# Hybrid block on one core: the index projections of the third and fourth group of tokens placed between the other projections

## The chip, the core and the metric

The kernel runs on one core of a Trainium2 chip. A core has five engines that run their own instruction streams and wait for each other through semaphores: TensorE (PE, matmuls; the loading of the stationary operand is shown apart as PEld), VectorE (DVE), ScalarE (ACT), GpSimd (POOL) and SyncE (SP, whose queue issues nearly all DMAs, in order). Matmul results land in PSUM banks, from which VectorE or ScalarE must read them before the bank is used again. All other tiles lie in SBUF. The metric is the time of one execution on the device in microseconds, less is better.

## What is computed

One layer of a streaming encoder on 2048 tokens of 1024 channels. The part that matters here is the combined input projection and the indexer:

```python
proj = x @ w_in[l]
q, c_kv, q_idx, w_idx, k_idx, pool_in, gate_logits = jnp.split(proj, PROJ_SPLITS, axis=-1)
q = apply_partial_rope(q.reshape(B, S, N_HEADS, D_LATENT), cos_q, sin_q)
k_lat = apply_partial_rope(c_kv, cos_q, sin_q)
q_idx = apply_partial_rope(q_idx.reshape(B, S, IDX_HEADS, IDX_DIM), cos_i, sin_i)
k_idx = apply_partial_rope(k_idx, cos_i, sin_i)
# per block of 128 queries:
rel = jax.nn.relu(jnp.einsum('bqhd,bsd->bqhs', qib, k_idx) * idx_scale)
idx_score = jnp.einsum('bqh,bqhs->bqs', wib * head_w_scale, rel)
_, sel = lax.top_k(jnp.where(admissible, idx_score, -inf), 256)
# pooling branch, gates
branch_b = multiscale_pool(pool_in, w_pool, pool_scale) @ w_pool_branch
gate_a, gate_b = jnp.split(jax.nn.sigmoid(gate_logits), 2, axis=-1)
```

Behind it come attention over the 256 selected keys of each query, the two branches under their gates, an output projection with layer norm, and a feed-forward part with a short convolution.

## The kernel before

All products are made in nearly full precision: each operand is split into a high and a low part (`split`: a rounded copy, then a subtraction), and `mm3` issues three matmuls, high by high, high by low and low by high. A split runs on ScalarE and VectorE, or with `pool=True` on GpSimd, in pieces of 256 columns.

Tokens are handled in four groups of 512 (`NG = 4`), each of four row blocks of 128. The projections run in these stages:

- *Index* (`proj_index`), per group: latent keys, index queries, index weights and index keys, 712 columns in three column thirds of 256, 256 and 200. x comes in four pairs of channel blocks; each pair is loaded, split, used for the first third and stored to DRAM in split form. Pair 0 of the next group is split ahead (`split_ahead`). The weights of all three thirds are loaded and split once (`Weights` object `wi`) and held in `wi_parts` over all four groups. `finish_index` makes the rotary part of keys and index queries on VectorE (tiles `rope`). `keys` transposes the keys on TensorE: eight transposes of 128x128 against `ident`, from which the index keys go to `kst`.
- *Pooling* (`proj_pool`), *queries* (`proj_q`) and *gates* (`proj_gates`), per group, in this order, from the stored x (`load_parts`). Their weights are split on GpSimd for group 0, kept in DRAM as `wp`, and only loaded for groups 1 to 3 (`self.ab`). `store_q` transposes the finished query rows; two pieces of each group are still to be transposed when gates begin. `pool_map` multiplies the four pooled channel groups by `wpool`: three matmuls each, then ScalarE and VectorE empty the bank. The pooled maps are used in the second half of gates.

Before, the order is: index 0, 1, 2, 3, then pooling, queries and gates of group 0, of group 1, of group 2 and of group 3, then attention. `keys` of a group is called behind the second third of the next index group; that of group 3 at the second step of group 0's pooling.

Beside these stages runs background work (`scores_and_selection`): for groups 0 and 1 together, then 2, then 3, index scores (matmuls of queries with `kst`, relu on ScalarE, weighted sums on VectorE) and the selection, a search for the threshold by bits with counts on VectorE and ScalarE, then the masks. It can begin for a set when `keys` of its last group has been called (`keyed`). `turn`, called at every step of a stage, lets it go on while a planned clock of VectorE and ScalarE is at most `SLACK` = 3 us behind TensorE's. A Tile scheduler then fixes each engine's order within these bounds. Four PSUM banks (`PS1`) serve the projections; SBUF has 42 slots of 4 KB per partition (`T`) for weights, x, scores and rows alike.

All instructions carry the line number of a wrapper (L153), so that groups are told apart by tile names and shapes.

Of the kernel before, what the change touches and what calls it, by code (L numbers as in the profile page):

```python
# [65 lines left out]
GROUPS = ((0, 1), (2,), (3,))  # L66
P1AT = (2, 2)
# [28 lines left out]
LASTK = 6  # L96
SCAN = 1.04
# [162 lines left out]
class Kern:  # L260
    def __init__(self, ctx, tc, a, out):
        self.clocks = Clocks()
        self.tc, self.nc, self.a, self.out = tc, PacedCore(tc.nc, self.clocks), a, out
        self.stores, self.older, self.bg, self.late = [], [], [], []
        self.const = ctx.enter_context(tc.tile_pool(name="const", bufs=1))
        self.big = ctx.enter_context(tc.tile_pool(name="big", bufs=42))
        self.mid = ctx.enter_context(tc.tile_pool(name="mid", bufs=8))
        self.sm = ctx.enter_context(tc.tile_pool(name="sm", bufs=4))
        self.early_pool = tc.alloc_tile_pool(name="early", bufs=1)
        self.late_pool = None  # L270
        self.p1 = ctx.enter_context(tc.tile_pool(name="p1", bufs=4, space=PSUM))
        self.p2 = ctx.enter_context(tc.tile_pool(name="p2", bufs=2, space=PSUM))
        self.dram = ctx.enter_context(tc.tile_pool(name="dram", bufs=1, space=bass.MemoryType.DRAM))
        self.n, self.shared = 0, True
        self.credit = self.seen = 0.0
# [156 lines left out]
    def setup(self):  # L432
# [28 lines left out]
        def cols(c0, n):  # L461
# [5 lines left out]
        self.wi = Weights(self, [cols(C_IDX, 256), cols(C_IDX + 256, 256), cols(C_IDX + 512, 200)], pool=False,  # L467
                          first=True)
# [86 lines left out]
    def proj_index(self, g, done):  # L555
# [3 lines left out]
        self.rows[g] = rows  # L559
        for c in range(3):  # L560
            if g == 0:
                self.wi_parts.append(self.wi.get(c))
            w = self.wi_parts[c]
            n = 256 if c < 2 else 200
            if c == 0:
# [7 lines left out]
                for _ in self.split_x(g, use):  # L573
                    if n == (XAT if g else 3) and g + 1 < NG:
                        self.load_x(g + 1)
                    n += 1
                    yield
                if g + 1 == NG:
                    self.ab.split(0)
                    self.load_parts(0, range(NFIRST))  # L580
            for rb in range(RB):
                if c == 0:
                    ps = accs[rb]
                else:
                    if (c, rb) == P1AT and g + 1 < NG:
# [17 lines left out]
            if c == 1 and done:  # L603
                done()

# [146 lines left out]
    def pool_map(self, g):  # L752
        nc = self.nc
        self.pm = []
        for k in range(4):
            t = self.pooled[k]
            ps = self.PS1()
            self.mm3(ps, self.wpool[:, 0, k], self.wpool[:, 1, k], t[:, 0], t[:, 1], True, True)
            o = self.T([P, 2, G], F32R)
            sc = self.pscale[:, k:k + 1]  # L760
            nc.scalar.activation(o[:, 0], ps, AF.Identity, scale=sc)
            nc.vector.scalar_tensor_tensor(o[:, 1], ps, sc, o[:, 0].bitcast(F32), op0=OP.mult, op1=OP.subtract)
            self.pm.append(o)
            yield 0.7

    def proj_gates(self, g):
        nc = self.nc
        base = g * self.nab + 6
        for j in range(4):
# [7 lines left out]
            for i in range(2):  # L777
# [9 lines left out]
                yield 5.2  # L787
        for j in range(4):
            w = self.ab.get(base + 4 + 2 * j)
            if j == 2:  # L790
                if g + 1 < NG:
                    self.load_parts(g + 1, range(NPRE))
                else:
                    self.attn_load()
# [5 lines left out]
            for i in range(2):  # L800
# [9 lines left out]
                yield 5.2  # L810
            if j == 3 and g + 1 < NG:
                self.load_parts(g + 1, range(NPRE, DC // 2))
# [1026 lines left out]
    def run(self):  # L1839
        self.qpend, self.rows, self.wi_parts, self.keyed, self.selected = [], {}, [], -1, 1  # L1840
# [9 lines left out]
        self.wi.raw[0] = [self.wi.load_one(0, 0)]  # L1850
        self.load_x(0, range(1, 2))
        self.wi.raw[0].append(self.wi.load_one(0, 1))
        self.load_x(0, range(2, DC // 2))
        self.split_ahead(0, 1)
        self.wi.split(0)
# [4 lines left out]
        for g in range(NG):  # L1860
            self.run_to_end(self.proj_index(g, done))
            while self.spill:
                self.store(*self.spill.pop(0))
            done = self.finish_index(g)
        self.load_parts(0, range(NFIRST, DC // 2))
        for g in range(NG):
            for i, step in enumerate(self.proj_pool(g)):
                if i == 1 and g == 0:
                    done()
                    self.wi_parts = None  # L1870
                self.turn(step)
            self.run_to_end(self.proj_q(g))
            self.run_to_end(self.proj_gates(g))
# [38 lines left out]
```

## Time and profile before

| | |
|---|---|
| time, three runs | median 3289.72 us (3289.57 to 3299.82) |
| time of the profiled execution | 3292.94 us |
| its span, from the first to the last instruction | 3291.2 us |
| mean granted TensorE clock | 0.982 |
| DMA | 745.68 MB, of it read from HBM 514.36 MB, written 228.23 MB |
| matmuls | 15918 |

The span is what the trace shows between the first and the last instruction; the execution's own time has 1.7 us around it. Windows of the trace are given in microseconds from the start of the span. A row of such a table has, for each engine, its busy time and its number of instructions, then the granted TensorE clock (1.00 is full speed) and the share of the DMA engines.

### The profile page before, as it was taken

The page shows a single profiled execution, that of the slowest core. Times are in us where ns is not written, and L with a number is a line of the kernel's source. Part 1 is how long each engine was busy: PE and PEld are TensorE (multiplying, and loading weights), DVE is VectorE, ACT ScalarE, POOL GpSimd, SP SyncE. Part 2 cuts the span into 40 slices and gives each one's busy share as a digit, 9 for nine tenths or more (in the row PEclk, how much of TensorE's full clock was granted, in tenths as well). Part 3 has the DMA queues.
Part 4 walks back from the last instruction along what each step waited for, and adds up shares of the span by engine and source line. Part 5 has one row for each costly group of instructions (what it writes and reads, how often), then busy time and mean ns, then how long its engine had stood idle before and what let it go on. Part 6 is the DMA issues. An engine that isn't in the chain of part 4 may idle for free. (4 is left out here: it accounts for less than half of the span.)

```text
span 3291.2 us, 46503 instructions
## 1 busy us (share of the span) xinstructions
PE 3157.8 (96%) x15918; PEld 2654.2 (81%) x15918; DVE 2417.7 (73%) x4271; ACT 1559.4 (47%) x2656; POOL 1279.9 (39%) x1314
## 2 busy tenths in 40 slices
PE   8988899999999899999999999999999999999998
PEld 8877688898898788788878877777778778888787
DVE  5588859986988777777766666666688865555797
ACT  3466537846777466666621133333343433222443
POOL 3139411020010688766641143443166511121673
PEclk9999899999999899999999999999999999999999
DMA  8457565653665444434464459899797665566984
GB/s 327 148 199 275 191 251 195 246 203 136 227 226 194 144 172 172 157 130 161 157 224 147 156 186 320 309 327 339 288 380 264 208 252 224 224 238 246 364 296 163
DMA packets 325675, 745.68 MB, mean 227 GB/s; under 512 B 30074, under 2 KB 115006, under 8 KB 325438
## 3 DMA queue, kind: packets, MB, share of 16 engines
q1 hardware_dynamic: 315646, 724.88, 61.5%
q10 hardware_dynamic: 9792, 17.83, 1.4%
q8 instruction: 126, 2.06, 0.3%
q14 instruction: 111, 0.91, 0.1%
HBM read 514.36 MB, written 228.23 MB: 226 GB/s over the span
## 5 line engine op out<-in xcount | busy, mean ns | idle before, releaser
L153 PE MATMUL p<-b,b 128*128 128x512 f32 (+3 forms) x12644 | 2783.7, 369 | 56.1 <-ACT b L153 24.4
L153 PEld LDWEIGHTS p<-b,b 128*128 128x128 f32 x12644 | 2175.7, 191 | 453.0 <-ACT b L153 25.0
L153 ACT ACTIVATE b<-p 128x512 fp32r<-128x512 f32 (+9 forms) x726 | 427.7, 612 | 653.6 <-PE p L153 627.0
L153 ACT ACTIVATE b<-b 128x1024 fp32r<-128x1024 f32 (+2 forms) x248 | 253.6, 1028 | 390.7 <-POOL b L153 136.4
L153 DVE TENSOR_TENSOR b<-b,b 128x1024 fp32r<-128x1024 f32 (+6 forms) x246 | 369.6, 1541 | 42.6 <-ACT b L153 39.8
L153 ACT ACTIVATE m<-b,F 128x1024 bf16<-128x1024 f32 (+3 forms) x352 | 345.8, 985 | 68.0 <-DVE F L153 43.8
L153 DVE TENSOR_SCALAR_CACHE_REDUCE m<-b,F 128x768 bf16<-128x768 f32 (+4 forms) x374 | 346.8, 949 | 11.8 <-DMA q<-m 9.9
L153 POOL TENSOR_TENSOR b<-b,b 128x256 fp32r<-128x256 f32 (+3 forms) x276 | 314.1, 1152 | 101.7 <-ACT b L153 84.9
L153 DVE TENSOR_TENSOR m<-m,p 128x512 f32<-128x512 f32 x176 | 120.3, 684 | 242.8 <-ACT b L153 182.6
L153 POOL TENSOR_TENSOR m<-b,b 128x512 f32<-128x512 f32 x99 | 140.2, 1425 | 337.4 <-issue 258.6
L153 DVE SCALAR_TENSOR_TENSOR b<-b,cw,b 128x1023 f32<-128x1023 f32 (+1 forms) x176 | 245.0, 1392 | 26.2 <-ACT b L153 25.1
L153 DVE TENSOR_TENSOR b<-p,b 128x512 fp32r<-128x512 f32 (+1 forms) x286 | 201.7, 714 | 72.3 <-ACT b L153 69.7
L153 POOL TENSOR_SCALAR b<-b 128x256 fp32r<-128x256 f32 (+3 forms) x216 | 125.8, 596 | 325.6 <-DMA b<-in_w_in_dram 122.8
L153 PE MATMUL p<-b 128*128 128x512 f32 x616 | 235.1, 393 | 5.8 <-ACT b L153 4.0
L153 POOL TENSOR_TENSOR b<-b,m 128x512 f32<-128x512 f32 x110 | 192.0, 1760 | 123.8 <-DMA m<-in_w_ffn_down_dram 74.0
L153 PE MATMUL p<-ident,b 128*128 128x128 f32 x1456 | 213.1, 274 | 24.8 <-ACT b L153 13.5
L153 DVE CUSTOM_DVE_ANT_0 b<-p,b 128x1024 f32<-128x1024 f32 (+7 forms) x192 | 174.2, 909 | 65.8 <-PE p L153 64.5
L153 PEld LDWEIGHTS p<-ident,b 128*128 128x128 f32 x1456 | 174.2, 141 | 58.7 <-ACT b L153 16.5
L153 ACT ACTIVATE b<-b,mx 128x1024 f32<-128x1024 f32 (+7 forms) x192 | 171.5, 896 | 69.7 <-DVE mx L153 63.7
L153 ACT ACTIVATE m<-p 128x512 f32<-128x512 f32 (+1 forms) x180 | 104.9, 594 | 193.6 <-PE p L153 178.9
L153 DVE SCALAR_TENSOR_TENSOR b<-b,ws,b 128x768 f32<-128x768 f32 (+5 forms) x154 | 159.8, 1065 | 40.6 <-ACT b L153 38.6
L153 PE MATMUL p<-kst,b 128*128 128x384 f32 (+3 forms) x656 | 150.6, 359 | 4.1 <-ACT b L153 2.6
(130 smaller groups left out, 2360.8 us busy)
## 6 DMA issues: line engine op xcount, KB each, us to landing
b<-uw SPq DMA_DIRECT2D x308, 512.0 KB, 6.5
b<-wp SPq DMA_DIRECT2D x192, 512.0 KB, 5.8
uw<-l SPq DMA_DIRECT2D x98, 512.0 KB, 3.0
b<-in_w_ffn_down_dram SPq DMA_DIRECT2D x154, 256.0 KB, 5.3
b<-h SPq DMA_DIRECT2D x154, 256.0 KB, 5.3
wp<-b SPq DMA_DIRECT2D x64, 512.0 KB, 5.2
uw<-b SPq DMA_DIRECT2D x56, 512.0 KB, 3.5
h<-m SPq DMA_DIRECT2D x110, 256.0 KB, 5.9
```

The lines of the kernel that those rows point to most:

```text
L153: return f(*args, **kw)
```

## The change

The list `STAGES` sets the order now: index 0 and 1, the other projections ("mix") of group 0, index 2, mix 1, index 3, mix 2, mix 3. As the index weights are no longer held, they are loaded and split again for index 2 and index 3, on GpSimd (`pool=g > 0`). `load_x` and the first splits of x for these groups are called in the second half of the gates ahead of them, and the loads of the stored x for the next pooling inside and behind them. The key transposes that precede a pooling stage come at its sixth step (`KEYS_AT = 5`), the query transposes left over at the second and third of the first four gate projections' weights, and the four pooling maps one at a time behind the gate projections number 4 to 7 (`PM_AT`). While projections run, every fourth split that was meant for GpSimd goes to ScalarE and VectorE (`self.turns % 4`).

```diff
+STAGES = (("index", 0), ("index", 1), ("mix", 0), ("index", 2), ("mix", 1), ("index", 3), ("mix", 2), ("mix", 3))
+KEYS_AT = 5
+PM_AT = (4, 5, 6, 7)
...
-        if pool:
+        self.turns += 1
+        if pool and (not self.shared or self.turns % 4):
...
-        self.wi = Weights(self, [cols(C_IDX, 256), cols(C_IDX + 256, 256), cols(C_IDX + 512, 200)], pool=False,
-                          first=True)
+        index = [cols(C_IDX, 256), cols(C_IDX + 256, 256), cols(C_IDX + 512, 200)]
+        self.wi = {g: Weights(self, index, pool=g > 0, first=g == 0)
+                   for (kind, g), before in zip(STAGES, (None,) + STAGES) if kind == "index" and before != (kind, g - 1)}
...
+        straight = after == ("index", g + 1)
         for c in range(3):
-            if g == 0:
-                self.wi_parts.append(self.wi.get(c))
+            if g in self.wi:
+                self.wi_parts[c] = self.wi[g].get(c)
...
-                if g + 1 == NG:
-                    self.ab.split(0)
-                    self.load_parts(0, range(NFIRST))
+                if not straight:
+                    if after[1] == 0:
+                        self.ab.split(0)
+                    self.load_parts(after[1], range(NFIRST))
...
+            if not straight:
+                self.wi_parts[c] = None
...
+    def pool_map(self, k):
+        t = self.pooled[k]
+        ps = self.PS1()
+        self.mm3(ps, self.wpool[:, 0, k], self.wpool[:, 1, k], t[:, 0], t[:, 1], True, True)
...
-            if j == 3:
-                yield from self.pool_map(g)
-            if self.qpend and j < 2:
+            if self.qpend and 1 <= j < 3:
                 self.store_q()
...
-                yield 5.2
+                if 2 * j + i + 1 in PM_AT:
+                    yield 2.6
+                    self.pool_map(len(self.pm))
+                yield 2.6
...
-                if g + 1 < NG:
-                    self.load_parts(g + 1, range(NPRE))
+                if g + 1 == NG:
+                    self.attn_load()
+                elif after[0] == "index":
+                    self.load_x(after[1])
+                    self.wi[after[1]].load(0)
                 else:
-                    self.attn_load()
+                    self.load_parts(g + 1, range(NPRE))
...
+                if after[0] == "index":
+                    self.wi[after[1]].split(0)
+                    self.split_ahead(after[1], 1)
+                else:
+                    self.load_parts(g + 1, range(NPRE, DC // 2))
...
-        for g in range(NG):
-            self.run_to_end(self.proj_index(g, done))
-            while self.spill:
-                self.store(*self.spill.pop(0))
-            done = self.finish_index(g)
-        self.load_parts(0, range(NFIRST, DC // 2))
-        for g in range(NG):
+        for (kind, g), after in zip(STAGES, STAGES[1:] + (None,)):
+            if kind == "index":
+                self.run_to_end(self.proj_index(g, done, after))
+                while self.spill:
+                    self.store(*self.spill.pop(0))
+                done = self.finish_index(g)
+                if after[0] == "mix":
+                    self.load_parts(after[1], range(NFIRST, DC // 2))
+                continue
             for i, step in enumerate(self.proj_pool(g)):
-                if i == 1 and g == 0:
+                if i == KEYS_AT and done:
                     done()
-                    self.wi_parts = None
+                    done = None
```

How this moves instructions is seen in each engine's order. The first place is TensorE at the pooling maps of group 0. In the names `p` is a PSUM bank, `b` a slot of SBUF, `wpool` the pooling map's weights. Before:

```order
L153 MATMUL p_1140_4540<-b_2861,b_4298 128x512
L153 MATMUL p_1140_4540<-b_2862,b_4298 128x512
L153 MATMUL p_1140_4540<-b_2861,b_4299 128x512
L153 MATMUL p_1168_4631<-b_3338,wpool_586 128x512 x3
L153 MATMUL p_1171_4641<-b_3516,wpool_586 128x512 x3
L153 MATMUL p_1178_4662<-b_3745,wpool_586 128x512 x3
L153 MATMUL p_1180_4669<-b_4032,wpool_586 128x512 x3
L153 MATMUL p_1184_4681<-b_2210,b_4459 128x512
```

Now, at the first of them:

```order
L156 MATMUL p_834_3158<-b_1414,b_2914 128x512
L156 MATMUL p_834_3158<-b_1413,b_2915 128x512
L156 MATMUL p_853_3223<-b_2000,wpool_586 128x512 x3
L156 MATMUL p_866_3255<-ident_84,b_2689 128x128 x4
L156 MATMUL p_868_3263<-ident_84,b_2689 128x128 x4
L156 MATMUL p_870_3271<-b_1066,b_3051 128x512
L156 MATMUL p_870_3271<-b_1067,b_3051 128x512
```

Four maps in a row, each with a bank of its own, have become one map between two gate projections; behind this first one stand query transposes, and the next map follows 24 matmuls later.

The second place is TensorE at key transposes ahead of a pooling stage (`ident` against `m`). Before, behind index 3, where the three matmuls are the last of 24 of group 0's pooling:

```order
L153 MATMUL p_700_2898<-b_2853,b_2190 128x512
L153 MATMUL p_700_2898<-b_2854,b_2190 128x512
L153 MATMUL p_700_2898<-b_2853,b_2191 128x512
L153 MATMUL p_701_2923<-ident_84,m_2763 128x128
L153 MATMUL p_702_2924<-ident_84,m_2764 128x128
```

Now, behind index 2, where they are the last of 48 of group 1's pooling:

```order
L156 MATMUL p_1369_5102<-b_5089,b_4254 128x512
L156 MATMUL p_1369_5102<-b_5090,b_4254 128x512
L156 MATMUL p_1369_5102<-b_5089,b_4256 128x512
L156 MATMUL p_1374_5176<-ident_84,m_4991 128x128
L156 MATMUL p_1375_5177<-ident_84,m_4992 128x128
```

The transposes stand 24 matmuls later than they did, behind index 2 and behind index 3 alike.

The third place is VectorE at the start of index 2, which is now behind the gates of group 0. The first row is the last product of these gates (`m`), the last is the split of index 2's second x pair; between them stand rows of the selection of groups 0 and 1 (`F` the threshold, `c` the counts, the others small working tiles), shown in part:

```order
L156 TENSOR_TENSOR m_4433<-p_1236_4451,m_4433 128x512
L156 SCALAR_TENSOR_TENSOR ab_4548<-t_4549 128x2
L156 TENSOR_SCALAR m_4762,c_4734<-b_2082,F_4471 128x896
L156 TENSOR_SCALAR ab_4548<-ab_4548 128x2
L156 SCALAR_TENSOR_TENSOR ab_4785<-F_4471 128x4
...
L156 TENSOR_TENSOR t_4786<-t_4786,ab_4785 128x4
L156 TENSOR_SCALAR tn_4787<-t_4786 128x4
L156 TENSOR_TENSOR b_4518<-b_4036,b_4517 128x1024
```

Before, the splits of index 2's four x pairs stood together among the rotary rows of index 1:

```order
L153 TENSOR_TENSOR rope_1311<-b_924,cos_547 128x16
L153 TENSOR_TENSOR rope_1313<-b_924,sin_548 128x16
L153 TENSOR_TENSOR b_1246<-b_960,b_1245 128x1024
L153 TENSOR_TENSOR b_1404<-b_962,b_1403 128x1024
L153 TENSOR_TENSOR b_1440<-b_964,b_1439 128x1024
L153 TENSOR_TENSOR b_1476<-b_966,b_1475 128x1024
```

The second to fourth of these splits moved from there to behind a gate product and 14 rows of selection.

More of the change, by code (lines that the diff above doesn't have):

```diff
@@ L553, in rope, with proj_index @@
         nc.vector.tensor_tensor(o2, ts[2], ts[3], op=OP.add)
-    def proj_index(self, g, done):
+    def proj_index(self, g, done, after):
         nc = self.nc
@@ L573, in proj_index @@
                 for _ in self.split_x(g, use):
-                    if n == (XAT if g else 3) and g + 1 < NG:
+                    if n == (XAT if g else 3) and straight:
                         self.load_x(g + 1)
@@ L584, in proj_index @@
                 else:
-                    if (c, rb) == P1AT and g + 1 < NG:
+                    if (c, rb) == P1AT and straight:
                         self.split_ahead(g + 1, P1N)
@@ L750, in lazy_step, with proj_gates @@
             self.lazy.pop(0)()
-    def pool_map(self, g):
+    def pool_map(self, k):
         nc = self.nc
[L754 to L766, printed above, removed]
+        t = self.pooled[k]
+        ps = self.PS1()
+        self.mm3(ps, self.wpool[:, 0, k], self.wpool[:, 1, k], t[:, 0], t[:, 1], True, True)
+        o = self.T([P, 2, G], F32R)
+        sc = self.pscale[:, k:k + 1]
+        nc.scalar.activation(o[:, 0], ps, AF.Identity, scale=sc)
+        nc.vector.scalar_tensor_tensor(o[:, 1], ps, sc, o[:, 0].bitcast(F32), op0=OP.mult, op1=OP.subtract)
+        self.pm.append(o)
+    def proj_gates(self, g, after):
         nc = self.nc
         base = g * self.nab + 6
+        self.pm = []
         for j in range(4):
             w = self.ab.get(base + j)
-            if j == 3:
-                yield from self.pool_map(g)
-            if self.qpend and j < 2:
+            if self.qpend and 1 <= j < 3:
                 self.store_q()
@@ L809, in proj_gates @@
                 self.after(DG, gate)
-                yield 5.2
+                if 9 + 2 * j + i in PM_AT:
+                    yield 2.6
+                    self.pool_map(len(self.pm))
+                yield 2.6
             if j == 3 and g + 1 < NG:
-                self.load_parts(g + 1, range(NPRE, DC // 2))
+                if after[0] == "index":
+                    self.wi[after[1]].split(0)
+                    self.split_ahead(after[1], 1)
+                else:
+                    self.load_parts(g + 1, range(NPRE, DC // 2))
             if j == 3 and g + 1 == NG:
@@ L1839, in run @@
     def run(self):
-        self.qpend, self.rows, self.wi_parts, self.keyed, self.selected = [], {}, [], -1, 1
+        self.qpend, self.rows, self.wi_parts, self.keyed, self.selected = [], {}, {}, -1, 1
         self.early, self.xr, self.xraw = {}, {}, {}
@@ L1849, in run @@
         self.setup()
-        self.wi.raw[0] = [self.wi.load_one(0, 0)]
+        self.wi[0].raw[0] = [self.wi[0].load_one(0, 0)]
         self.load_x(0, range(1, 2))
-        self.wi.raw[0].append(self.wi.load_one(0, 1))
+        self.wi[0].raw[0].append(self.wi[0].load_one(0, 1))
         self.load_x(0, range(2, DC // 2))
         self.split_ahead(0, 1)
-        self.wi.split(0)
+        self.wi[0].split(0)
         self.split_ahead(0, 1)
@@ L1859, in run @@
         done = None
[L1860 to L1866 removed]
+        for (kind, g), after in zip(STAGES, STAGES[1:] + (None,)):
[7 more added lines that the diff above has]
+                continue
             for i, step in enumerate(self.proj_pool(g)):
[L1868 removed]
+                if i == KEYS_AT and done:
                     done()
[L1870 removed]
+                    done = None
                 self.turn(step)
             self.run_to_end(self.proj_q(g))
[L1873 removed]
+            self.run_to_end(self.proj_gates(g, after))
         self.shared = False
```

3 lines of the change are left out of this document (1 added, 2 removed).

## The prediction

> **What bounds the kernel now.** I read the page's head first, then busy time by stage, then the idle time that stands before single instructions in TensorE's timeline.
>
> ```profile
> span 3291.2 us, 46503 instructions
> PE 3157.8 (96%) x15918; PEld 2654.2 (81%) x15918; DVE 2417.7 (73%) x4271; ACT 1559.4 (47%) x2656; POOL 1279.9 (39%) x1314
> ```
>
> TensorE is busy for 96% of the span, so a reordering can win idle time, and time in which matmuls run at a lowered clock, and nothing else. Where both lie is seen by stage. In order the rows are: index group 1; index 2; index 3; group 0's pooling projection, its query projection, its gates; group 1's pooling and query projections together, its gates; group 2's gates; group 3's pooling and query, its gates; the start of attention; the rest.
>
> ```profile
> core 0: us, PE busy (x) PEld busy (x) DVE busy (x) ACT busy (x) POOL busy (x), PEclk, DMA share, GB/s
> 46.00:80.80 34.80, 34.80 (x300) 34.80 (x299) 16.49 (x88) 11.18 (x31) 0.00 (x0) 1.00 0.80 303
> 80.80:129.80 49.00, 44.89 (x351) 42.93 (x351) 21.80 (x75) 18.67 (x49) 0.00 (x0) 1.00 0.26 92
> 129.80:196.10 66.30, 62.83 (x451) 59.70 (x450) 48.11 (x59) 38.96 (x59) 15.80 (x20) 1.00 0.57 198
> 196.10:232.80 36.70, 26.49 (x108) 20.51 (x107) 33.32 (x105) 19.51 (x42) 21.47 (x44) 0.81 0.57 199
> 232.80:290.70 57.90, 51.81 (x402) 50.89 (x400) 56.24 (x152) 39.83 (x85) 44.86 (x78) 0.94 0.68 239
> 290.70:428.70 138.00, 120.80 (x508) 97.83 (x509) 117.92 (x295) 72.21 (x137) 84.52 (x145) 0.91 0.71 252
> 428.70:559.00 130.30, 122.26 (x770) 109.68 (x769) 97.16 (x178) 77.81 (x139) 18.20 (x18) 0.97 0.49 185
> 559.00:672.80 113.80, 113.67 (x511) 93.91 (x510) 101.79 (x342) 95.16 (x211) 0.67 (x4) 1.00 0.75 267
> 743.30:914.80 171.50, 171.50 (x791) 143.55 (x790) 138.94 (x238) 123.80 (x182) 0.68 (x4) 1.00 0.53 191
> 914.80:984.40 69.60, 69.60 (x498) 65.83 (x497) 61.88 (x165) 54.03 (x105) 11.45 (x14) 1.00 0.57 202
> 984.40:1118.70 134.30, 126.25 (x552) 103.76 (x551) 113.01 (x270) 76.53 (x142) 32.50 (x41) 0.94 0.55 188
> 1118.70:1163.00 44.30, 36.05 (x202) 28.77 (x201) 37.08 (x94) 27.47 (x70) 34.45 (x28) 0.96 0.30 99
> 1163.00:3291.00 2128.00, 2069.42 (x9710) 1699.34 (x9708) 1486.07 (x2019) 856.32 (x1314) 969.36 (x813) 0.99 0.66 235
> ```
>
> Some stages run clean (TensorE busy throughout, clock 1.00) and give yardsticks: an index group 34.8 us, pooling and queries 69.6, gates 113.8. Index scoring is mixed into others; its matmuls, the ones that read `kst`, have these busy times, in the stages index 2, index 3, pooling and queries 1, gates 2:
>
> ```profile
> 80.80:129.80 49.00, 9.25 (x32) 5.10 (x32) 0.69 (x1) 0.58 (x1) 1.00 0.26 92
> 129.80:196.10 66.30, 29.59 (x128) 20.97 (x128) 0.69 (x1) 0.59 (x1) 1.00 0.57 198
> 428.70:559.00 130.30, 50.66 (x240) 37.40 (x240) 0.00 (x0) 0.00 (x0) 0.97 0.49 185
> 743.30:914.80 171.50, 61.12 (x256) 46.82 (x256) 0.00 (x0) 0.00 (x0) 1.00 0.53 191
> ```
>
> Gates 2 has no idle time, so group 3's scoring costs 171.5 - 113.8 = 57.7 us there, 0.944 of its 61.12. By that factor groups 0 and 1 cost 36.7 us and group 2 costs 47.8. What each stage takes beyond its yardsticks is then: index 2 and 3, 49.0 + 66.3 - 69.6 - 36.7 = 9.0; pooling and queries 0, 36.7 + 57.9 - 69.6 = 25.0; gates 0, 24.2; pooling and queries 1, 130.3 - 69.6 - 47.8 = 12.9; gates 3, 20.5, of which 552 - 511 = 41 narrow matmuls of attention, 0.116 us each as in index 1 (34.8/300), are 4.8 us of work, so 15.7; start of attention, 44.3 - 36.05 = 8.2. That is 95 us which an order of the same work could win at most. Behind 1163 us every engine's order is the same in both kernels, so those 2128 us stay.
>
> **What the change removes.** The waits it aims at, in TensorE's timeline (start, length, instruction, and in brackets the idle time before it with what ended it): the key transposes of index group 3, the last query transposes, the pooling maps with the gate matmul behind them, and the first scores of attention.
>
> ```profile
> 203.88 0.30 PE L153 MATMUL p<-ident,m 128*128 128x128 f32 x1 [1.77 <-DVE m L153]
> 208.75 0.48 PE L153 MATMUL p<-ident,m 128*128 128x128 f32 x1 [3.98 <-DVE m L153]
> 213.09 0.85 PE L153 MATMUL p<-ident,m 128*128 128x128 f32 x2 [2.76 <-DVE m L153]
> 294.60 1.12 PE L153 MATMUL p<-ident,b 128*128 128x128 f32 x4 [2.86 <-ACT b L153]
> 334.35 0.97 PE L153 MATMUL p<-b,wpool 128*128 128x512 f32 x3 [1.21 <-ACT m L153]
> 338.82 1.65 PE L153 MATMUL p<-b,wpool 128*128 128x512 f32 x3 [3.50 <-ACT m L153]
> 345.60 1.65 PE L153 MATMUL p<-b,wpool 128*128 128x512 f32 x3 [5.13 <-ACT m L153]
> 350.62 5.60 PE L153 MATMUL p<-b,b 128*128 128x512 f32 x15 [3.38 <-DVE b L153]
> 1099.80 3.78 PE L153 MATMUL p<-b,b 128*128 128x128 f32 x10 [4.16 <-ACT b L153]
> ```
>
> *Keys.* They now stand behind 48 pooling matmuls instead of 24, 48 x 113.8/511 = 10.7 us after the index group. In these two windows (rope rows of VectorE alone) a rope row took 14.60/44 = 0.33 us while GpSimd was splitting weights, and 11.58/82 = 0.14 us while it was idle.
>
> ```profile
> 46.00:84.00 38.00, 11.58 (x82) 1.00 0.77 290
> 196.10:215.00 18.90, 14.60 (x44) 0.72 0.16 59
> ```
>
> Behind index 2 and 3 GpSimd has next to nothing to do now, so the ropes need about 6 us where they needed 15, and fit into the 10.7. The 8.5 us of quoted waits and the clock of 0.81 over 36.7 us (7.0 lost) go.
>
> *Pooling and queries 0.* The scoring of groups 0 and 1 moves in here, as group 2's stands in pooling and queries 1 already. I take that stage's excess, 12.9, for the 9.0 + 25.0 of now: **-21**. Ends: all 34 stay lost (0), or all go (-34).
>
> *Maps.* Each map now stands between two gate projections, 24 matmuls (5.3 us) apart, so its bank is emptied under cover of the next projection. The quoted waits for maps, for the matmul behind them and for the last query transposes, which move by one projection as well, are 16.1 us, and the clock of 0.91 over 138 us is worth 12.4; together more than the 24.2 of the yardstick, so clock and waits overlap. I leave 5 for banks that wait for ScalarE: **-19**, ends -24 and -8.
>
> **What it adds.** *The start of index 2.* Its x pairs 1 to 3 are split on ScalarE and VectorE as they are used. VectorE's order shows 13 narrow rows and a wide one between the last gate product and the first of these splits.
>
> ```profile
> 133.04 2.35 DVE L153 TENSOR_TENSOR b<-b,b 128x1024 fp32r<-128x1024 f32 x2
> 218.20 0.16 DVE L153 SCALAR_TENSOR_TENSOR g<-wd,wa 128x4 f32<-128x4 f32 x1
> 1092.74 0.70 DVE L153 TENSOR_SCALAR fx<-cg 128x2 f32<-128x2 f32 x1
> ```
>
> A split is 1.2 us, the wide row I count alike, the product as half; 13 narrow rows take 2.1 to 9.1. So the split ends 5.1 to 12.1 us after gates 0, and TensorE has 24 matmuls of pair 0, 24 x 34.8/300 = 2.8 us, to cover it. It waits 2.3 to 9.3 us, the middle 5.8, then an estimated 1 us for each of pairs 2 and 3 behind three and five mask rows, and 1.2 for a lowered clock: **+9**. Ends +2, and +18: 9.3, twice 2, and the clock of 0.81 over some 25 us (4.7). *The start of index 3*: the split stands right behind the gate product, 0.6 + 1.2 us against 2.8: **+2**, ends 0 and 9 as above. *Keys of group 3*: two blocks of mask rows stand among the ropes: **+3**, ends 0 and 9. *Scores of group 3*: some 160 of their 288 matmuls and transposes leave the clean gates 2 for queries 2; 12.9 x 160/288: **+7**, ends 0 and 13.
>
> *Reloaded index weights*: 12 loads and 12 splits of 512 KB or less. Rows: GpSimd's pieces during gates 0, the landing time of such a load, and TensorE's total wait for GpSimd.
>
> ```profile
> L153 POOL TENSOR_TENSOR b<-b,b 128x256 fp32r<-128x256 f32 x72 | 54.9, 783 | 0.0
> L153 POOL TENSOR_SCALAR b<-b 128x256 fp32r<-128x256 f32 x72 | 32.4, 467 | 10.4 <-DMA b<-in_w_in_dram 6.7 <-DMA b<-in_w_pool_branch_dram 3.6
> b<-in_w_in_dram SPq DMA_DIRECT2D x32, 512.0 KB, 6.5
> PE p L153 <- POOL b L153: 2.2, 4, 0.9
> ```
>
> A tile is 4 x (0.783 + 0.467) = 5.0 us, two make a column third in 10.0, and TensorE uses a third in 34.8/3 = 11.6. GpSimd keeps ahead if it begins before the stage does, and it may, since its loads are queued while gates run: 0. Without this cover the first reloaded third waits 6.5 + 10.0 - 11.6 = 5 us in each stage, inside the ends above. The quarter of the splits that goes to ScalarE and VectorE gives each 13 more, 13 x 1.2 = 16 us of VectorE over 1118 us; hidden in its idle time, else again inside those ends. SyncE gets the 12 loads; the first rows of x for group 1's pooling stand behind a mask store there, which is weighed below.
>
> *Gates 3 and start of attention.* Selection ends earlier against TensorE, no selection row is left behind the first scores, and the q and k splits wait behind less: half of 15.7 and of 8.2 go: **-8** and **-4**; ends 0 and -24 together.
>
> **Sum.** -21 - 19 + 9 + 2 + 3 + 7 - 8 - 4 = -31 us. The profiled execution took 3292.9 us (3291.2 and 1.7 around it), 3.2 more than the median of 3289.7; with the same difference the forecast is **3259 us**.
>
> **Rivals.** *VectorE becomes the bound.* From index 2 to gates 0 it is busy 277.4 us; without index 3 some 261. At gates 0's share, 117.92/138 = 0.854, that needs 305 us, against 347.9 - 34.8 = 313 now: 8 saved where I have 31 (21 + 19 - 9). Sum -8: 3282 us, no change. For it: 0.85 to 0.97 busy at 196 to 429. Against: 101.79/113.8 = 0.89 in gates 1 with TensorE never idle. The Trainium skill, SBUF — State Buffer, "Who interferes with whom", says that GpSimd and a VectorE row with two SBUF inputs exclude each other for a whole instruction. It speaks against splitting reloaded weights on GpSimd. The rope rows above agree (0.33 and 0.14 us); by it alone the ropes of both groups would gain nothing, 2 x 44 x 0.19 = 17 us, and the sum would be -14. But these ropes need the last third's rows, so the reloaded weights are split by then.
>
> *VectorE reaches the index stages late*, slower. The splits of x in index 2 and 3 now stand behind gate products and selection; before, index groups followed each other. The masks' stores, and the loads of x behind them on SyncE, wait with them.
>
> ```profile
> SPq L366 <- DVE b L153: 409.2, 68, 24.2
> ```
>
> The longest such wait of a store is 24.2 us. If VectorE is that late at both starts, TensorE waits 24.2 and loses 7.0 of clock twice, 62 us, of which 11 are counted: +51 - 31 = +20, 3310 us. It decides from about 20 us of lateness at each. Against: the planner stops selection at 3 us of planned backlog (`SLACK`), and through index 2 and 3 the clock stayed at 1.00 beside scoring.
>
> **Chances.** My forecast's case (3228 to 3280) 0.66; still more won, towards the sum of the good ends (-80), 0.06; VectorE as the bound, 0.15; VectorE late, 0.13. About 0.3% (10 us) is what a measurement can tell from no change: faster 0.72, same 0.15, slower 0.13. The range 3228 to 3300 leaves out the best 0.06 and most of the late case.
>
> **What would show it.** Right: no wait of over 2 us before `wpool` matmuls and key transposes; pooling and queries 0 at about 69.6 + 36.7 + 13 us; gates 0 near 119; clock near 1.00 there; one wait of 2 to 9 us before index 2's second x pair. Wrong: TensorE waiting for VectorE at both index starts by over 15 us; gates 0 still above 130 with VectorE over 0.9 busy; or TensorE waiting for GpSimd or loads in index 2 and 3.

## The result, and the profile after

The changed kernel takes 3266.55 us (median of 4 runs, 3263.37 to 3273.83); before, in the same series, 3293.33 (4 runs, 3289.57 to 3299.82). The ratio is 0.992, interval 0.9893 to 0.9946, so it is 26.8 us faster, and the forecast was 31 (3259 us, from a time before of 3289.7). The profiled execution took 3269.0 us with a span of 3266.9, 24.3 less than before. The number came out; the reason given for it did not, as the experiments show.

The page's head of the changed kernel (busy time, share of the span, instructions of each engine):

```profile
span 3266.9 us, 46556 instructions
PE 3149.2 (96%) x15918; PEld 2651.6 (81%) x15918; DVE 2412.6 (74%) x4284; ACT 1570.9 (48%) x2669; POOL 1272.7 (39%) x1306
```

Busy time by stage, in the new order: index 1; pooling 0, queries 0, gates 0; index 2; pooling and queries 1, gates 1; index 3; pooling and queries 2, gates 2; pooling and queries 3, gates 3; start of attention; the rest.

```profile
core 0: us, PE busy (x) PEld busy (x) DVE busy (x) ACT busy (x) POOL busy (x), PEclk, DMA share, GB/s
47.60:82.40 34.80, 34.80 (x300) 34.78 (x298) 7.99 (x56) 6.08 (x21) 2.76 (x6) 1.00 0.88 317
82.40:118.40 36.00, 31.24 (x147) 24.17 (x146) 23.99 (x64) 13.46 (x33) 12.27 (x26) 1.00 0.71 250
118.40:209.40 91.00, 83.62 (x569) 77.73 (x568) 84.21 (x132) 56.27 (x91) 58.61 (x74) 0.96 0.42 148
209.40:336.40 127.00, 118.50 (x508) 97.34 (x509) 115.33 (x347) 104.51 (x199) 67.36 (x122) 0.96 0.79 284
336.40:380.30 43.90, 38.03 (x290) 37.23 (x288) 37.99 (x98) 13.09 (x32) 25.51 (x34) 0.88 0.81 291
380.30:505.10 124.80, 118.97 (x777) 110.09 (x776) 94.24 (x185) 72.41 (x127) 16.40 (x17) 0.97 0.45 164
505.10:623.20 118.10, 115.51 (x512) 95.33 (x511) 107.28 (x349) 100.13 (x219) 7.98 (x14) 0.99 0.72 252
623.20:661.10 37.90, 35.63 (x289) 35.27 (x288) 36.97 (x136) 27.25 (x68) 5.97 (x15) 0.95 0.75 251
661.10:764.90 103.80, 102.74 (x665) 94.31 (x665) 83.07 (x130) 49.24 (x75) 15.46 (x16) 1.00 0.47 162
764.90:907.00 142.10, 142.10 (x640) 117.22 (x639) 121.34 (x257) 109.69 (x177) 0.66 (x4) 1.00 0.64 226
907.00:976.60 69.60, 69.60 (x497) 65.83 (x496) 63.28 (x168) 53.21 (x104) 11.50 (x14) 1.00 0.56 196
976.60:1099.70 123.10, 119.55 (x552) 98.96 (x551) 101.33 (x225) 64.77 (x117) 20.45 (x23) 1.00 0.61 210
1099.70:1138.50 38.80, 37.49 (x228) 31.90 (x227) 29.93 (x101) 30.70 (x79) 33.02 (x31) 1.00 0.36 121
1138.50:3266.90 2128.40, 2063.62 (x9684) 1694.61 (x9682) 1476.08 (x2006) 851.55 (x1302) 958.87 (x811) 0.99 0.66 235
```

Gates 0 has fallen from 138.0 to 127.0 us and gates 3 from 134.3 to 123.1; index 2 is 43.9 instead of a yardstick of 34.8; the rest is 2128.4 against 2128.0. VectorE is 0.91 busy in gates 0 (115.33/127.0), and TensorE's clock there is 0.96 where it was 0.91.

### The profile page after: what moved, and what is told of

The parts are those of the page before. It is cut to its first block, busy times and chain, and to the rows that moved or that the text cites. A ratio compares the mean times of both kernels' runs of the same rounds, so it can differ in the third digit from the quotient of the medians.

```text
span 3266.9 us, 46556 instructions
## 1 busy us (share of the span) xinstructions
PE 3149.2 (96%) x15918; PEld 2651.6 (81%) x15918; DVE 2412.6 (74%) x4284; ACT 1570.9 (48%) x2669; POOL 1272.7 (39%) x1306
## 5 line engine op out<-in xcount | busy, mean ns | idle before, releaser
L156 ACT ACTIVATE b<-p 128x512 fp32r<-128x512 f32 (+8 forms) x726 | 428.2, 613 | 660.4 <-PE p L156 636.5
L156 ACT ACTIVATE b<-b 128x1024 fp32r<-128x1024 f32 (+2 forms) x261 | 267.0, 1028 | 402.5 <-POOL b L156 134.8
L156 DVE TENSOR_TENSOR b<-b,b 128x1024 fp32r<-128x1024 f32 (+6 forms) x259 | 378.4, 1494 | 53.5 <-ACT b L156 50.7
L156 POOL TENSOR_TENSOR b<-b,b 128x256 fp32r<-128x256 f32 (+3 forms) x272 | 322.1, 1198 | 102.7 <-ACT b L156 85.9
L156 DVE TENSOR_TENSOR b<-p,b 128x512 fp32r<-128x512 f32 (+1 forms) x286 | 201.8, 713 | 69.6 <-ACT b L156 66.9
```

The source lines that it names most:

```text
L156: return f(*args, **kw)
```

## The experiments

The changed kernel stands in the table with the four runs of the result; each other kernel was timed in rounds beside the kernel before (5 to 12 runs). The ratio is to the kernel before in the same series; "us" is (ratio - 1) x 3293.3. "Gates 0" is from the stage's first matmul to the first of the next stage, in one profiled execution, and so may differ by up to a microsecond from the windows above. "Long row" is the longest of the short rows of selection (128x4 or 128x2) on VectorE in gates 0.

| kernel | order | keys, queries, maps | moved splits | ratio (interval) | us | gates 0 | long row |
|---|---|---|---|---|---|---|---|
| before | straight | as before | none | 1 | 0 | 137.8 | 5.29 |
| changed | new | spread | a quarter | 0.9920 (0.9893 to 0.9946) | -26 | 126.2 | 1.33 |
| e1_straight_spread | straight | spread | a quarter | 0.9906 (0.9889 to 0.9924) | -31 | 128.2 | 0.77 |
| e2_order_alone | new | as before | a quarter | 0.9925 (0.9912 to 0.9939) | -25 | 124.6 | 0.79 |
| e3_maps_burst | new | maps together | a quarter | 0.9935 (0.9917 to 0.9953) | -21 | 132.0 | 7.88 |
| e4_keys_early | new | keys early | a quarter | 0.9933 (0.9919 to 0.9947) | -22 | 129.5 | 0.84 |
| f1_turns_alone | straight | as before | a quarter | 0.9932 (0.9920 to 0.9944) | -22 | 122.9 | 0.77 |
| f2_no_turns | new | spread | none | 1.0009 (0.9997 to 1.0020) | +3 | 137.1 | 10.48 |
| f3_straight_spread_no_turns | straight | spread | none | 0.9970 (0.9960 to 0.9980) | -10 | 133.3 | 11.61 |
| h1_other_quarter | straight | as before | another quarter | 0.9974 (0.9960 to 0.9989) | -9 | 129.6 | 0.72 |
| h2_half | straight | spread | a half | 0.9927 (0.9914 to 0.9939) | -24 | 125.7 | 0.69 |
| g1_hold_selection | new | spread | a quarter | 0.9939 (0.9927 to 0.9951) | -20 | 126.3 | 1.32 |
| g2_x_ahead | new | spread | a quarter | 0.9939 (0.9927 to 0.9951) | -20 | 127.8 | 5.28 |

**Order against spreading.** e1 puts the index groups back, e2 takes the spreading back:

```diff
 e1
-STAGES = (("index", 0), ("index", 1), ("mix", 0), ("index", 2), ("mix", 1), ("index", 3), ("mix", 2), ("mix", 3))
+STAGES = (("index", 0), ("index", 1), ("index", 2), ("index", 3), ("mix", 0), ("mix", 1), ("mix", 2), ("mix", 3))
 e2
-KEYS_AT = 5
-PM_AT = (4, 5, 6, 7)
+KEYS_AT = 1
+PM_AT = ()
...
-            if self.qpend and 1 <= j < 3:
+            if j == 3:
+                for k in range(4):
+                    self.pool_map(k)
+                    yield 0.7
+            if self.qpend and j < 2:
```

> The order of before (index 0 to 3, then the other projections), with the spreading of the change kept: keys of group 3 at the sixth pooling step, query transposes at the second and third gate weights, maps behind gate projections 4 to 7. Theory A (the gain comes from what stood close together at pooling 0 and gates 0, that is keys and maps): most of the gain remains, 15 to 30 us below before; gates 0 falls from 138 to 120-128 us, pooling and queries 0 from 94.6 to 80-86. Theory B (the gain comes from where the index groups and the scores stand): within 8 us of before, gates 0 above 132.

> The new order, without the spreading: keys at the second pooling step, query transposes at the first two gate weights, the four maps together ahead of the last gate weights. Theory A: 15 us or more of the 27 are lost, the time is within 12 us of before; gates 0 is back above 134 us. Theory B: 18 to 28 us below before, as the changed kernel.

Both theories failed at once. Spreading without the new order won 31 us, as theory A said (its range ended at 30); the new order without spreading won 25, as theory B said; together they win 26. Either the two replace each other, or a part that both still contained does the work.

**Single pieces of the spreading.** e3 sets only `PM_AT = ()` and the loop at `j == 3`, e4 only `KEYS_AT = 1`.

> The changed kernel with the four pooling maps together ahead of the last gate weights, as before. Theory A: 8 to 16 us above the changed kernel, that is 11 to 19 below before; gates 0 goes from 127 to 133-138 us, gates 3 from 123 to 126-130, gates 1 and 2 up to 3 us each. Theory B: within 4 us of the changed kernel.

> The changed kernel with the key transposes at the second pooling step. Theory A: TensorE waits for rotated keys again, 6 to 15 us at pooling 0, where GpSimd splits weights beside the ropes, and 0 to 5 us at pooling 1 and 2, where it does not; 6 to 20 us above the changed kernel. Theory B: within 4 us of the changed kernel.

Both are 4 to 5 us above the changed kernel, between the ranges of the two theories, and their intervals overlap with its own, so neither piece is shown to matter by time. In the traces, e3's gates 0 is 5.8 us longer, but it has a VectorE row of 7.88 us (explained below) as well as the maps together, so that the two are not separated; its gates 3 is not longer with the maps together but shorter (117.6 us against 121.7). And the first places that e4 was expected to lose at are no worse: pooling and queries 0 took 122.8 us against 126.4. At pooling 2, where 0 to 5 us were expected, TensorE waited 2.21, 4.98 and 1.23 us before key transposes, the last two for rotated keys.

**The small edit.** f1 is in effect the kernel before with one condition of the change, f2 the changed kernel without that condition:

```diff
 f1 against before
-        if pool:
+        self.turns += 1
+        if pool and (not self.shared or self.turns % 4):
 f2 against the changed kernel
-        if pool and (not self.shared or self.turns % 4):
+        if pool:
```

> The order, the keys, the query transposes and the maps all as before; of the change only one part is left: while projections run, every fourth split meant for GpSimd goes to ScalarE and VectorE. Straight order with spreading gained 33 us and the new order without spreading 25, though together they gain 27, so they are either substitutes (theory S: each takes away the same waits at pooling 0 to gates 0) or share a part that neither took out, which is this one (theory T). S: within 5 us of before, gates 0 at 133-138 us. T: 15 to 25 us below before, gates 0 at 124-130 us.

> The changed kernel, but all splits meant for GpSimd stay there. S: within 5 us of the changed kernel. T: 10 to 25 us above it, with TensorE waiting for GpSimd's splits or for rotated keys between pooling 0 and gates 0, or in index 2 and 3.

The condition alone wins 22 us (interval 18 to 26), and all the rest of the change without it wins nothing (+3, interval -1 to +7). Theory T holds in what it said of the times of f1; f2 is further above the changed kernel than it said (29 us, not 10 to 25), and the waits are not those that it named, as will be seen. The counter runs over all splits; 11 tiles are moved (1226 GpSimd instructions on f1's page where before has 1314, eight to a tile). In gates 0, f1 and f2 in one row each:

```profile
287.90:410.80 122.90, 116.30 (x510) 95.00 (x509) 113.80 (x298) 75.64 (x141) 59.91 (x103) 0.99 0.77 282
...
212.10:349.20 137.10, 117.09 (x509) 96.14 (x509) 128.54 (x338) 99.10 (x191) 86.71 (x162) 0.93 0.75 269
```

GpSimd's busy time is 60 us against 87, the clock 0.99 against 0.93, TensorE's idle time 6.6 us against 20.0. These two differ in order and spreading too; in the pairs that differ by this condition alone TensorE's idle time in gates 0 is 17.2 us before against 6.6 in f1, and 20.0 in f2 against 7.5 in the changed kernel. How does a helper that TensorE hardly ever waits for cost it 10 to 13 us? In f2's timelines of VectorE, ScalarE and TensorE (start, length, instruction, idle time before it with what ended it):

```profile
230.76 10.48 DVE L156 SCALAR_TENSOR_TENSOR g<-wd,wa 128x4 f32<-128x4 f32 x1
...
243.35 0.83 ACT L156 ACTIVATE m<-b,F 128x640 bf16<-128x640 f32 x1 [10.85 <-DVE F L156]
...
251.62 0.57 ACT L156 ACTIVATE m<-p 128x512 f32<-128x512 f32 x1
...
252.25 1.12 PE L156 MATMUL p<-ident,b 128*128 128x128 f32 x4 [13.61 <-ACT m L156]
```

A row of four elements per partition, whose operands were ready, lasts 10.48 us beside an unbroken run of split pieces on GpSimd (it normally takes 0.15). The next limit `F` of the selection is late by that, ScalarE stands idle for 10.85 us before the count that reads it, and the emptying of a PSUM bank (`m<-p`) is queued behind that count and four more. TensorE waits 13.61 us for the bank. Before shows the same at the pooling maps; here its VectorE, the last row of GpSimd's run that had begun at 290, and ScalarE:

```profile
324.09 5.29 DVE L153 SCALAR_TENSOR_TENSOR g<-wd,wa 128x4 f32<-128x4 f32 x1
...
345.27 3.56 DVE L153 SCALAR_TENSOR_TENSOR g<-wd,wa 128x4 f32<-128x4 f32 x1
...
327.93 1.43 POOL L153 TENSOR_TENSOR b<-b,b 128x256 fp32r<-128x256 f32 x2
...
329.82 0.83 ACT L153 ACTIVATE m<-b,F 128x640 bf16<-128x640 f32 x1 [4.83 <-DVE F L153]
```

The first row ends at 329.38, GpSimd's run at 329.36; GpSimd's next piece begins 6.72 us later, when a weight has landed. The longest row is f3's (this kernel comes below), here with the last row of GpSimd's run and the next:

```profile
308.70 11.61 DVE L156 SCALAR_TENSOR_TENSOR g<-wd,wa 128x4 f32<-128x4 f32 x1
...
318.87 1.43 POOL L156 TENSOR_TENSOR b<-b,b 128x256 fp32r<-128x256 f32 x2
337.30 0.77 POOL L156 TENSOR_SCALAR b<-b 128x256 fp32r<-128x256 f32 x2 [17.00 <-DMA b<-in_w_pool_branch_dram]
```

All six rows of over 3 us in gates 0 of the thirteen kernels are this instruction, `g<-wd,wa`. Five of them end within 0.02 us of the last piece of a run of GpSimd, behind which GpSimd stands idle for 5 us or more; f2's alone ends inside a run.

In the kernel before, the three waits ahead of `wpool` matmuls and the one behind them, from which the prediction priced the maps, stand in the 21 us behind that row, and the second long row, 3.56 us, ends at 348.82, 1.8 us before the last of them does.

The 121 short rows of gates 0 took 41.1 us together before and 120 of them 34.5 in f1; without its two long rows before has 32.2. So between these two kernels it is the two long rows, and not the holding-up of all short rows, that went away. Between f2 and the changed kernel both did: 161 rows took 63.1 us and 43.7, and f2 has 52.6 without its long row.

Two limits of this reading. Waits of this kind remain without a long row: 5.80 us in e4's gates 0, 4.27 in the changed kernel's. And gates 0 is not all of the gain: it is 14.9 of the 21.3 us by which f1's profiled execution is below that of before, and 10.9 of the 29 between f2 and the changed kernel, where pooling 2 to gates 3 are 16 us shorter. What the moved quarter does there was not followed up.

**Is it these rows, and how many splits?** h1 moves another quarter, h2 a half (on e1), f3 none (on e1):

```diff
 h1 against f1
-        if pool and (not self.shared or self.turns % 4):
+        if pool and (not self.shared or self.turns % 4 != 2):
 h2 against e1
-        if pool and (not self.shared or self.turns % 4):
+        if pool and (not self.shared or self.turns % 2):
 f3 against e1
-        if pool and (not self.shared or self.turns % 4):
+        if pool:
```

> Before in all but one part, as in the run with only the quarter of the splits moved, but another quarter of the splits is moved (9 or 10 tiles, as there). Theory P (GpSimd's unbroken runs of split pieces hold up VectorE's short rows, TensorE waits behind; any shortening of the runs helps): 12 to 25 us below before, gates 0 at 121-129 us, and no short VectorE row of over 3 us in gates 0. Theory C (the moved quarter by chance avoided two unlucky rows): within 8 us of before, with rows of over 3 us in other places.

> The straight order with spreading, and every second split meant for GpSimd moved instead of every fourth. P: GpSimd's runs are shorter still, gates 0 below 126 us (128.2 with a quarter), the time 0 to 8 us below the 3263 of the quarter. If VectorE and ScalarE are now the limit, with some 10 more splits of 1.2 us each: 5 to 12 us above it.

> The straight order with keys, query transposes and maps spread, all splits meant for GpSimd left there. If spreading is worth what it adds to the moved quarter (33 against 22): 5 to 14 us below before, and the new order then costs about as much, since both together without the quarter are 0. If spreading only pays together with the moved quarter: within 5 us of before.

h1 wins 9 us, between the two ranges. Its gates 0 fell by 8.2 us to 129.6, just outside theory P's range, with no short row above 0.72 us, so the second quarter removes the long rows as well. It also bears on a rival: the moved splits change the order in which the scheduler sets VectorE's and ScalarE's work, and this alone might shorten gates 0. Of VectorE's 293 instructions in gates 0 before, 289 stand in the same order in h1, but only 243 in f1. So 8.2 us went with the long rows while the order stayed, and what the rest of f1's 14.9 owes to its other order was not tested. TensorE at the maps of h1:

```profile
333.15 2.26 PE L156 MATMUL p<-b,wpool 128*128 128x512 f32 x9
340.94 1.65 PE L156 MATMUL p<-b,wpool 128*128 128x512 f32 x3 [5.53 <-ACT m L156]
```

With the maps together and no long row, one such wait is left. h1's index 0 is 6.3 us longer than f1's (44.4 against 38.1), as one of the splits it moves stands at the very start. ScalarE's timeline there:

```profile
8.55 1.06 ACT L156 ACTIVATE b<-b 128x1024 fp32r<-128x1024 f32 x1 [0.27 <-DMA b<-in_xT_dram]
19.92 2.95 ACT L156 ACTIVATE b<-b 128x1024 fp32r<-128x1024 f32 x3 [10.32 <-DMA b<-in_w_in_dram]
```

ScalarE stands 10.32 us before a weight that has not landed, with the splits of x in line behind it. h2 has the same loss at the start (43.0 us), the second shortest gates 0 of the straight kernels (125.7 us, as P said), and is 7 us above e1 in time, with intervals that overlap. That is the other theory's figure, but the start alone is 5.1 us longer than e1's (37.9), so h2 does not decide between them. f3 wins 10 us: spreading is worth about the same without the moved quarter (10) as with it (31 - 22 = 9, with intervals that just overlap), and the new order costs 13 on top of it without the quarter (f3 against f2, intervals apart), 5 with it (e1 against the changed kernel, intervals overlapping). f3's profiled execution was the fastest of its twelve (3274.6 us, median 3283.5), so its stage lengths flatter it.

Over all thirteen kernels, the five with a row of over 3 us in gates 0 need 127.8 to 137.8 us there (mean 133.6), the eight without 122.9 to 129.6 (mean 126.6). All three kernels with no split moved have such a row in their one profiled execution, and two of the ten with moved splits (e3 and g2): moving them makes these rows rarer, it does not exclude them. g2's row stands at the end of gates 0, and no wait of over 2 us follows it within 20 us.

**The rows by themselves.** m1 runs VectorE's short rows and a wide count beside unbroken runs of pieces on GpSimd.

```python
nc.gpsimd.tensor_scalar(hi[:, c], src[:, c], 1.0, 1.0, op0=OP.mult, op1=OP.mult)
nc.gpsimd.tensor_tensor(lo[:, c], src[:, c], hi[:, c].bitcast(F32), op=OP.subtract)
...
nc.vector.tensor_scalar(junk, src[:, 0:512], src[:, 8:9], None, op0=OP.is_gt, op1=OP.add, accum_out=wd[:, r % 4:r % 4 + 1])
nc.vector.scalar_tensor_tensor(g, wa, 2.0, src[:, 0:4], op0=OP.mult, op1=OP.subtract)
nc.vector.tensor_scalar(h, g, 511.0, 256.0, op0=OP.is_lt, op1=OP.mult)
```

> Only a measurement: nothing of the layer is computed, the output is zeros. VectorE runs 24 times a wide count (128x512, one SBUF input), a short row with two SBUF inputs (128x4) and a short row with one (128x4), four times: beside an idle GpSimd, beside an unbroken run of split pieces (rounding copy and subtraction, 128x256) on GpSimd, beside the copies alone, and beside the subtractions alone. P: 0.15-0.17 us for a short row beside the idle GpSimd, 0.3 to 0.8 on average beside split pieces, some rows as long as several pieces (over 2 us), the wide count unchanged at 0.74. If VectorE's long rows in the kernel are something else (its own semaphores, the scheduler): all short rows stay at 0.15-0.2 us beside all runs.

Groups of instructions in three stretches: GpSimd idle (87 to 103 us), copies and subtractions (28 to 70), subtractions alone (103 to 133). The last figure ahead of the second bar is the mean of one in ns.

```profile
L60 DVE TENSOR_SCALAR_CACHE_REDUCE junk<-src 128x512 bf16<-128x512 f32 x19 | 13.9, 730 | 0.0
L65 DVE TENSOR_SCALAR h<-g 128x4 int32<-128x4 f32 x20 | 2.3, 154 | 0.0
L64 DVE SCALAR_TENSOR_TENSOR g<-wa,src 128x4 f32<-128x4 f32 x18 | 2.0, 147 | 0.0
...
L60 DVE TENSOR_SCALAR_CACHE_REDUCE junk<-src 128x512 bf16<-128x512 f32 x40 | 29.3, 733 | 0.0
L65 DVE TENSOR_SCALAR h<-g 128x4 int32<-128x4 f32 x40 | 9.9, 291 | 0.0
L64 DVE SCALAR_TENSOR_TENSOR g<-wa,src 128x4 f32<-128x4 f32 x40 | 8.8, 258 | 0.0
...
L53 POOL TENSOR_TENSOR lo<-src,hi 128x256 fp32r<-128x256 f32 x40 | 27.3, 720 | 1.3 <-DVE wa L58 1.3
L60 DVE TENSOR_SCALAR_CACHE_REDUCE junk<-src 128x512 bf16<-128x512 f32 x24 | 17.6, 734 | 0.0
L65 DVE TENSOR_SCALAR h<-g 128x4 int32<-128x4 f32 x24 | 8.3, 388 | 0.0
L64 DVE SCALAR_TENSOR_TENSOR g<-wa,src 128x4 f32<-128x4 f32 x24 | 7.7, 360 | 0.0
```

Short rows are held up, wide counts are not (0.73 throughout), and no short row in these stretches is longer than one piece of GpSimd: 0.71 us at most. Beside the copies alone, a short row took 0.28 us with two inputs and 0.21 with one on average. P had expected 0.3 to 0.8 beside the full run, a little more than the 0.26 and 0.29 there, and rows of over 2 us, which did not come. So the ordinary hold is shown by itself; the hold over many pieces is not reproduced. In the kernel it is read off the traces alone, where five of the six long rows end with GpSimd's run; what decides when it occurs stays open.

**The start of index 2.** g1 issues no selection between the last gate weights and the first third of index 2 and 3, g2 splits three pairs of x ahead:

```diff
 g1
+        self.hold = False
...
-        while self.bg and self.clocks.backlog() < SLACK and self.credit > 0:
+        while self.bg and not self.hold and self.clocks.backlog() < SLACK and self.credit > 0:
...
+                self.hold = False
...
+                    self.hold = True
 g2
-                    self.split_ahead(after[1], 1)
+                    self.split_ahead(after[1], 3)
```

> The changed kernel, but no selection is issued from the last gate products ahead of index 2 and 3 until their x has been used for the first column third. If the start of index 2 (43.9 us for 34.8) waits because VectorE runs selection counts ahead of the last gate products, which hold two of the four banks, and ahead of the splits, index 2 falls to 35-38 us and index 3 from 37.9 to 35-36.5; 5 to 11 us less in all if the held selection finds room later, 0 to 4 less if it comes back as excess in the stages behind. If the splits of x wait for something else (a load), both stay as they are.

> The changed kernel with three pairs of x split ahead of index 2 and 3 instead of one, so that VectorE's splits stand before the last gate products and the selection counts that go with them. If the late splits set the start of index 2, as forecast, it falls from 43.9 to 36-39 us. If it is the banks that the last gate products hold, it stays above 41 us, since those products now stand behind more VectorE work.

TensorE at the start of index 2 in the changed kernel, with VectorE's last two gate products and the split of x pair 1:

```profile
340.79 0.98 PE L156 MATMUL p<-b,b 128*128 128x256 f32 x6 [2.55 <-DVE m L156]
343.92 2.72 PE L156 MATMUL p<-b,b 128*128 128x256 f32 x11 [2.16 <-DVE m L156]
347.80 1.43 PE L156 MATMUL p<-b,b 128*128 128x256 f32 x5 [1.16 <-DVE b L156]
...
340.05 0.68 DVE L156 TENSOR_TENSOR m<-p,m 128x512 f32<-128x512 f32 x1
343.19 0.68 DVE L156 TENSOR_TENSOR m<-p,m 128x512 f32<-128x512 f32 x1
346.52 1.23 DVE L156 TENSOR_TENSOR b<-b,b 128x1024 fp32r<-128x1024 f32 x1
```

The first two waits end with the two gate products, which empty banks that the new group needs; only the third ends with the split. g2 agrees: with the splits earlier, index 2 took 45.7 us, not 36 to 39. g1 settles nothing at index 2 (44.6): the same counts, issued ahead of the hold, still stand before the products in VectorE's order. At index 3, where the hold took effect, the stage fell from 37.9 to 35.0. Both kernels are 6 us slower than the changed one, with intervals that overlap.

## Why the prediction was right, and where its reasons were wrong

Stage lengths from one execution of each kernel (us, first matmul to first matmul, the last row to the end of the last matmul) show which part moved what:

| | before | f1: quarter alone | f2: all but the quarter | changed |
|---|---|---|---|---|
| index 0 and 1 | 72.0 | 72.7 | 74.4 | 75.2 |
| index 2, 3, pooling and queries 0 | 210.2 | 207.3 | 213.4 | 208.2 |
| gates 0 | 137.8 | 122.9 | 137.1 | 126.2 |
| pooling, queries, gates 1 | 244.2 | 242.2 | 243.3 | 242.9 |
| pooling, queries, gates 2 | 241.9 | 242.0 | 255.8 | 245.9 |
| pooling, queries, gates 3 | 202.5 | 200.5 | 197.3 | 191.2 |
| attention to the end | 2161.8 | 2162.3 | 2153.8 | 2156.5 |

- *The moved quarter, priced at 0 ("hidden in its idle time").* **This is the step that failed.** It is worth 22 us by itself, some 15 of them in gates 0. The prediction counted what the splits cost the engines that receive them, and not what it frees VectorE from when GpSimd runs less.
- *Maps, -19.* Gates 0 fell by 11, but not for that reason: with maps and query transposes spread and no quarter moved it stayed at 137.1, and with the maps together and a quarter moved it fell to 122.9. The waits quoted ahead of `wpool` matmuls were priced as the maps' own, but stand behind a VectorE row of 5.29 us which held up ScalarE. With the maps together and no long row the longest wait there is 2.35 us in f1 and 5.53 in h1, so some share of the maps' is not excluded.
- *Pooling and queries 0, -21.* These stages took 127.0 us, 20.7 over 69.6 + 36.7, where 12.9 was taken; 34.0 before, so -13. A size that was off: group 2's excess of 12.9 did not carry over to these stages, in which GpSimd is busy with splits; whether that is the reason was not tested.
- *Keys.* No wait at key transposes above 1.04 us in the changed kernel, as said. At pooling 0 this was not due to their later step (e4). At pooling 2 it was, and "keys of group 3, +3, ends 0 and 9" reached its far side in f2, where one wait of 7.97 us stands behind mask rows among the ropes.
- *Start of index 2, +9.* Measured 43.9 - 34.8 = 9.1, with waits of 2.55, 2.16 and 1.16; the size was right, but the two longer of the three waits are for banks, not for the split. *Index 3, +2*: 37.9 - 34.8 = 3.1.
- *Scores of group 3, +7, and keys, +3.* Pooling, queries and gates 2 together took 4.0 more, not 10.
- *Gates 3, -8*: 123.1 - 113.8 - 4.8 = 4.5 over its yardstick where it was 15.7, so -11. Selection that ends earlier is not needed for it: straight kernels with spreading (e1, f3) have 121.7 and 121.6 us, f1 without it 130.9. With the maps together and the query transposes late it was shortest (e3, 117.6), with both early 125.7 (e2), whose first wait there is one of 3.39 us for transposes; this points to the query transposes. *Start of attention, -4*: 44.3 to 38.8, -5.5.
- *Reloaded weights, 0.* TensorE waits neither for GpSimd nor for a load in index 2 and 3 of the changed kernel; right.
- *The rivals.* VectorE was no bound: at 0.91 busy gates 0 still gave 11 us. VectorE was late at the index stages by 6 us and 2, not by 24. The Trainium skill (SBUF — State Buffer, "Who interferes with whom") says that a VectorE row with two SBUF inputs and a GpSimd instruction that reads SBUF exclude each other for a whole instruction, the later one blocking. m1 agrees (0.15 us alone, at most 0.71 beside a subtraction of 0.72), and by that rule alone the moved quarter would be worth next to nothing in f1, since without the two long rows gates 0's short rows took 32.2 us before and 34.5 in f1 (between f2 and the changed kernel, by the same reckoning, some 9). The kernel's rows of 3.56 to 11.61 us, through 7 to 22 pieces of GpSimd, go beyond it.
- *The signs.* Of those named for "right", the first alone holds (no wait of over 2 us before `wpool` matmuls and key transposes): pooling and queries 0 took 127 us, not about 119, gates 0 126, not near 119, at a clock of 0.96, and the wait for the split of index 2's second x pair was 1.16 us, where 2 to 9 had been named.

The terms of the sum that rest on order and spreading came to about 0 together (f2) where -31 was forecast, and the term left at 0 brought nearly what was forecast. That the total came out is therefore luck. The new order without spreading and without the moved quarter was not run, so what it costs alone stays open. The lowest of all times, 3262.6 us, belongs to e1, which leaves the index groups where they were; it is not told apart from the changed kernel (intervals 0.9889 to 0.9924 and 0.9893 to 0.9946).

## What to carry to other kernels

A wait that stands before an operation need not be that operation's cost: follow it back through the engine that ended it until a row is longer than its shape explains. A small edit inside a large reordering, above all one that relieves a helper engine, is to be priced by what it frees on the other engines as well, and run alone before the large part gets the credit. Where splits are moved to engines that run in order, those whose data lands late are left where they are.

## What the runs showed of the hardware

VectorE rows of four elements per partition lasted 3.56, 5.28, 5.29, 7.88, 10.48 and 11.61 us beside GpSimd's unbroken runs of split pieces, where 0.15 is usual. All but the one of 10.48 ended within 0.02 us of the end of a GpSimd run. In attention, a row of the same size (`rinv<-ssum`, about 0.18 as a rule) lasted 4.64 to 4.66 us in eight of the thirteen kernels, through four GpSimd instructions, and ended within 0.03 us of the end of the last. In the direct measurement, with as dense a run, rows were held by one piece only, and a short row with a single SBUF input as long as one with two (0.39 and 0.36 us on average beside subtractions), while a count of 512 elements with an accumulator was never lengthened.
